# Quadrant products of a two-block transformer kernel issued in rows, inverse transforms in pairs, forward transforms on the whole array

## The chip, the cores and the metric

The kernel runs on one core of a Trainium2 chip, as one launch. The metric is the device time of one execution in microseconds. The core's engines are told by the profile's names: PE (matrix products; PEld is its weight load), DVE (elementwise on vectors), ACT (activations), POOL, and SP, whose queue issues the weight loads.

## What is computed

512 tokens of 1024 features pass two blocks. The first is a conformer convolution (a product to 2048 columns with a gate, a depthwise convolution of width 31 inside segments of 64 tokens, a layer norm, a second product) and an MLP. The second has two layers: differential attention with a Fourier mix in layer 0, a short convolution in layer 1, and behind each a mixture of 16 experts, in which every expert takes its best 64 tokens.

```python
def rms_norm(x, g):
    xf = x.astype(jnp.float32)
    y = xf * lax.rsqrt(jnp.mean(xf * xf, axis=-1, keepdims=True) + EPS)
    return (y * g.astype(jnp.float32)).astype(x.dtype)
...
    u = dwconv(u.reshape(B * n_seg, L // n_seg, D), w_dw).reshape(B, L, D) + b_dw
    u = jax.nn.silu(layer_norm(u, ln_g, ln_b))
    return u @ w_pw2 + b_pw2
...
    aff = jax.nn.softmax(h.astype(jnp.float32) @ w_router.astype(jnp.float32), axis=-1)
    g, idx = lax.top_k(aff.swapaxes(1, 2), cap)
    xs = jax.vmap(lambda hb, ib: hb[ib])(h, idx)
    a = jax.nn.silu(jnp.einsum('becd,edf->becf', xs, w_gate)) * jnp.einsum('becd,edf->becf', xs, w_up)
    y = jnp.einsum('becf,efd->becd', a, w_down) * g[..., None].astype(h.dtype)
...
        x = x + g_m * y
        x = x + g_f * ec_moe(modulate_2(x, norm_ffn[l], sh_f, sc_f),
                             router_w[l], moe_w_gate[l], moe_w_up[l], moe_w_down[l])
```

The norms are over all 1024 features of a token; h of the router is the normed x.

## The kernel before

The activations are kept as X, 128 partitions by 8 feature blocks f by 512 tokens, so a sum over features is a sum over partitions and blocks. A framework orders the instructions of each engine from the program's text and its buffers; each engine works through its own row in that order, and waits by semaphores.

Dense products are three products each (`mm3`, L442 to L444): weight and input are split into a high and a low part by ACT (L435) and DVE (L436). They work on halves of the tokens, 256 columns, in most stages (L442, `128x256`), and on 512 columns in the convolution's.

A sum of squares over features (`sumsq`) is made of eight squares by ACT (`square`, L349; tile `sq`, four buffers) and eight products on PE (L351) with a block of 32 columns of ones. Block f goes to quadrant 32 * (f % 4) of the PSUM tile `sm`, so that four products in a row lie in four different quadrants. It is called in the second norm of block 1 (both halves), the norm of layer 0 (both halves, with 32 weighted columns in place of ones) and the norm of layer 1 (both halves).

In the output product of each layer (`mix_out`) each block of 128 features is added to X by DVE (L730) as soon as its dense product is done, and behind it `route_stat` adds to the token statistics of the router: a product of X with the router's weights (L1235, 32 columns, tile `wrg`) and the product of a square (L351), both in quadrant f % 4. Four groups of four blocks follow each other: half 0 of the tokens with f 0 to 3, then 4 to 7, then half 1. Behind half 0's last block `route_half` makes the router's softmax and, on DVE, the top-k (L1278 to L1281).

In `conv_half` (called for two halves of 256 tokens) the depthwise convolution is a transform: for each of four pieces (two tiles of 128 tokens, two halves of 512 features) PE transforms the two segments of 64 tokens (L690, a tile of 64 rows and 119 columns: the first segment in rows 0 to 63, the second in rows 64 to 127), DVE multiplies by the filter's transform (L693), and PE transforms back (L696, 119 rows, 64 columns: segment b into columns 64 * b of one tile). All these, and the squares' and router's products, are f32 and show as two MATMULs each in the trace.

The experts' weights are loaded through one queue of SP (L1411) into buffers that come free as PE's expert products (L1426) are done.

Of the kernel before, what the change touches and what calls it, by code (L numbers as in the profile page):

```python
# [153 lines left out]
class _Net:  # L154
# [173 lines left out]
    def sumsq(self, xs, t0, n, w=None):  # L328


        nc = self.nc
        ps = self.sm_ps()
        for f in range(KT):
            self.square(ps[:, :n], xs, f, t0, n, f < 4, f >= 4, None if w is None else w[:, f])
        s = self.tmp.tile([128, 256], F32, name="sqs", tag="sqs", bufs=1)
        nc.vector.tensor_copy(s[:, :n], ps[:, :n])
        m = 1 if w is None else 2
        for t in range(n // 128):
            nc.tensor.matmul(ps[:, 256 + m * t:256 + m * t + m], s[:, 128 * t:128 * t + 128],
                             self.cst("quad" if w is None else "quad2"), start=True, stop=True,  # L340
                             skip_group_check=True)
        out = ps[:, 256:256 + m * n // 128]
        return out if w is None else out.rearrange("p (t m) -> p t m", m=2)

    def square(self, ps, xs, f, t0, n, start, stop, w=None):

        nc = self.nc
        s = self.tmp.tile([128, 256], F32, name="sq", tag="sq", bufs=4)
        nc.scalar.activation(s[:, :n], xs[:, f, t0:t0 + n], AF.Square)  # L349
        q = 32 * (f % 4)  # L350
        nc.tensor.matmul(ps[q:q + 32], self.cst("ones")[:, :32] if w is None else w, s[:, :n], start=start, stop=stop,  # L351
                         skip_group_check=True)

    def rsqrt(self, ms, n, tag="rs"):

# [317 lines left out]
    def conv_half(self, hf, u, gf, bdw, zh, zl):  # L673

        nc = self.nc
        fo = _CO["dft"][0]
        cv = self.page().rearrange("p (t d) -> p t d", t=2)
        for i in range(2):
            t = 2 * hf + i

            sm = self.sml.tile([128, 3], F32, name="lns", tag="lns")
            prt = self.page()
            pr = prt[:119].rearrange("p (b d) -> p b d", b=2)
            for h in range(2):
                c = slice(512 * h, 512 * h + 512)
                ps = []
                for b in range(2):
                    p = self.mm_ps()
                    o, q = fo + 119 * b, slice(64 * b, 64 * b + 64)
                    nc.tensor.matmul(p[:119], self.cs[q, o:o + 119], u[q, t, c], start=True, stop=True)  # L690
                    ps.append(p)
                for b in range(2):
                    nc.vector.tensor_tensor(pr[:, b, c], ps[b][:119], gf[:, c], op=ALU.mult)  # L693
                o = self.sm_ps()
                for b in range(2):
                    nc.tensor.matmul(o[64 * b:64 * b + 64], self.cst("idft", 119), pr[:, b, c],  # L696
                                     start=True, stop=True, skip_group_check=True)
                nc.vector.tensor_tensor_reduce(cv[:, i, c], o, bdw[:, c], 1.0, 0.0 if h == 0 else sm[:, 0:1],
                                               ALU.add, ALU.add, sm[:, h:h + 1])

            nc.vector.tensor_scalar(sm[:, 1:2], sm[:, 1:2], -1.0 / D, None, op0=ALU.mult)
            nc.scalar.activation(prt[:, :D], cv[:, i], AF.Square, bias=sm[:, 1:2], accum_out=sm[:, 2:3])
            nc.vector.tensor_scalar(sm[:, 2:3], sm[:, 2:3], 1.0 / D, None, op0=ALU.mult)
            r = self.rsqrt(sm[:, 2:3], 1, tag="ln")
            nc.vector.tensor_scalar(cv[:, i], cv[:, i], sm[:, 1:2], r, op0=ALU.add, op1=ALU.mult)
            if i == 1:

                nc.scalar.activation(sm[:, 0:1], r, AF.Silu)
        for f0 in range(0, KT, 2):
            ps = self.sm_ps()  # L710
            for j in range(2):
                f = f0 + j
                for i in range(2):
                    o = 256 * j + 128 * i
                    nc.tensor.transpose(ps[:, o:o + 128], cv[:, i, 128 * f:128 * f + 128], self.cst("ident"))
            for j in range(2):
                f = f0 + j
                s = self.tmp.tile([128, T], F32, name="sl", tag="sl", bufs=2)
                nc.scalar.activation(s[:, :256], ps[:, 256 * j:256 * j + 256], AF.Silu,
                                     bias=self.vec("conv_ln_b", f), scale=self.vec("conv_ln_g", f))  # L720
                self.split(zh[:, f], zl[:, f], s[:, :256])
        if hf == 1:
            with self.logs_table():
                nc.scalar.copy(self.sml.tile([128, 1], F32, name="done0", tag="lns1"), s[:, :1])
# [438 lines left out]
    def mix_out(self, l, src, xh, xl, key, w=None, last_head=False):  # L1163

        if w is None:
            w = list(self.pieces(self.wload(src[:, :512])))
        src = [src[:, :512], src[:, 512:]]
        mids = [None] * 4
        if last_head:

            w = w[:2] + w[3:] + w[2:3]
            mids[0] = lambda: self.head_norm(5, self.sm_ps())
        route = self.stop >= 7 + 2 * l
        if route:
            self.lg, self.sqb = self.sm_ps(), self.sm_ps()
            chain = [self.route_half(t0, n) for t0, n in self.AB]
            r = []
            mids[2] = lambda: r.append(next(chain[0]))

        for i in range(4):  # L1180
            add = self.add_to_x(self.mods[key], 4 * (i % 2))

            def ev(j, ps, gi, t0, n):
                add(j, ps, gi, t0, n)
                if route:
                    self.route_stat(4 * (i % 2) + j, t0, n)

            nxt = self.wload(src[(i + 1) % 2]) if i < 3 else []
            it = []
            self.dense_f(w, self.groups(xh, xl, self.AB[i // 2:i // 2 + 1]), ev, mids[i],  # L1190
                         lambda: it.extend(self.pieces(nxt)))
            w = it
            if route and i == 2:
                next(chain[0])
        if route:
            r.append(next(chain[1]))
            next(chain[1])
            next(chain[0], None)
            for i in range(2):
                self.token_major(*self.AB[i], r[i])  # L1200
            next(chain[1], None)
        self.dump("d_y%d" % l, self.X)
# [27 lines left out]
    def route_stat(self, f, t0, n):  # L1230

        q = 32 * (f % 4)
        ts = slice(t0, t0 + n)
        first = f < 4 and t0 == 0
        self.nc.tensor.matmul(self.lg[q:q + 32, ts], self.wr[:, f], self.X[:, f, ts], start=first, stop=(f >= 4),  # L1235
                              skip_group_check=True)
        self.square(self.sqb[:, ts], self.X, f, t0, n, first, f >= 4)

    def route_half(self, t0, n):

# [177 lines left out]
    def product(self, name, l, j, lhs, mid=None):  # L1418

        ps = [self.mm_ps(), self.mm_ps()]  # L1420
        for k in range(KT):
            if k % 2 == 0:
                w = [self.eload(self.rows(name, l, j + 8 * b)[:, k:k + 2]) for b in range(2)]
            for n in range(2):
                for b in range(2):
                    self.pe(self.nc.tensor.matmul(ps[n][64 * b:64 * b + 64], lhs[:, k, 64 * b:64 * b + 64],  # L1426
                                                  w[b][k % 2][:, 512 * n:512 * n + 512],
                                                  start=(k == 0), stop=(k == KT - 1), skip_group_check=True))
            if mid and k < 6:
                mid(k)  # L1430
        return ps
# [203 lines left out]
```

## Time and profile before

| | before |
|---|---|
| median of 3 runs | 2148.46 us (2144.57 to 2150.37) |
| profiled execution | 2149.96 us |
| its span | 2148.2 us |
| mean granted clock of PE | 0.984 |
| PE busy | 2043.2 us, 95% |
| DVE busy | 1004.7 us, 47% |
| ACT busy | 558.5 us, 26% |
| moved by DMA | 581.26 MB |

The span is the profiled execution from its first to its last instruction; busy times are of that one execution. The median is over executions without a profile. A granted clock of 1.00 is the full clock of PE.

### The profile page before, as it was taken

Reading aid. Unit: us, or ns where it says so; the run is one execution under the profiler, and the core shown is the slowest. Engines: PE = TensorE matmul, PEld = TensorE weight load, DVE = VectorE, ACT = ScalarE, POOL = GpSimd, SP = SyncE. Lnnn points to the kernel's source line nnn. Section 1 sums busy time; section 2 is a strip of 40 time slices with the busy share of each in tenths; the row PEclk is TensorE's granted clock in tenths of the full one; section 3 lists DMA queues with packets and bytes.
Section 4 is the critical chain, followed back from the end, with each engine's and each line's share of the span. In section 5 each row is a group of like instructions: output and inputs, shape, how many; then the busy total and the mean of one; then the engine's idle time right before and its main releaser. Section 6 shows DMA issues by size and latency. Waiting matters only on the chain. (4 is left out here: it accounts for less than half of the span.)

```text
span 2148.2 us, 26989 instructions
## 1 busy us (share of the span) xinstructions
PE 2043.2 (95%) x10986; PEld 1353.0 (63%) x10986; DVE 1004.7 (47%) x1998; ACT 558.5 (26%) x1035; POOL 18.0 (1%) x20
## 2 busy tenths in 40 slices
PE   6999999999999989989999999979998999999998
PEld 4758888788888978865444434428887544444443
DVE  3878995787575469661222212235356122121221
ACT  3344534243343359630000000023233000000001
POOL 0000000000000000000000000010000000000000
PEclk8999999999999999999999999989999999999999
DMA  9726486588411253448999999992254799999997
GB/s 357 260 80 214 168 292 184 189 290 257 151 47 33 81 142 94 173 161 321 411 420 421 421 421 421 420 356 68 97 215 157 293 404 421 421 421 420 421 421 279
DMA packets 157979, 581.26 MB, mean 271 GB/s; under 512 B 12385, under 2 KB 21505, under 8 KB 111008
## 3 DMA queue, kind: packets, MB, share of 16 engines
q1 hardware_dynamic: 157344, 579.00, 70.7%
q8 instruction: 86, 1.41, 0.3%
q10 hardware_dynamic: 320, 0.52, 0.1%
q14 instruction: 37, 0.30, 0.0%
q0 software_dynamic: 192, 0.03, 0.0%
HBM read 571.50 MB, written 2.11 MB: 267 GB/s over the span
## 5 line engine op out<-in xcount | busy, mean ns | idle before, releaser
L442 PE MATMUL mm<-b,wh 128*128 128x512 f32 (+1 forms) x1136 | 391.4, 346 | 0.6 <-ACT ao L1138 0.5
L443 PE MATMUL mm<-b,wh 128*128 128x512 f32 (+1 forms) x1136 | 391.6, 345 | 0.0
L444 PE MATMUL mm<-b,wl 128*128 128x512 f32 (+1 forms) x1136 | 388.2, 343 | 0.0
L1426 PE MATMUL mm<-w,xs 128*64 128x512 f32 x1152 | 263.8, 600 | 13.2 <-DMA w<-w_u 13.2
L436 DVE TENSOR_TENSOR wl<-w,wh 128x1024 fp32r<-128x1024 f32 x160 | 194.1, 1221 | 168.2 <-ACT wh L435 167.0
L435 ACT CAST wh<-w 128x1024 fp32r<-128x1024 f32 x164 | 170.4, 1049 | 341.7 <-PE mm L443 264.4
L442 PEld LDWEIGHTS mm<-b,wh 128*128 128x128 f32 x1136 | 215.6, 190 | 39.2 <-issue 10.4
L443 PEld LDWEIGHTS mm<-b,wh 128*128 128x128 f32 x1136 | 216.0, 190 | 33.9 <-issue 8.7
L444 PEld LDWEIGHTS mm<-b,wl 128*128 128x128 f32 x1136 | 215.4, 190 | 27.5 <-issue 2.9
L1444 DVE TENSOR_TENSOR ea<-mm,ea 128x512 f32<-128x512 f32 x32 | 22.1, 691 | 395.8 <-PE mm L1426 348.9
L1426 PE MATMUL mm<-b,xs 128*64 128x512 f32 x864 | 198.4, 594 | 3.7 <-DMA b<-w_u 3.5
L1426 PEld LDWEIGHTS mm<-w,xs 128*64 128x64 f32 x1152 | 84.7, 138 | 175.1 <-issue 140.3
L249 DVE SCALAR_TENSOR_TENSOR w<-w,sc 128x512 f32<-128x512 f32 x252 | 184.0, 748 | 4.9 <-DMA w<-ada_w 1.6
L1426 PEld LDWEIGHTS mm<-b,xs 128*64 128x64 f32 x864 | 69.0, 137 | 123.8 <-issue 102.2
L1381 PEld LDWEIGHTS sm<-o,b 128*128 128x128 f32 x1024 | 118.8, 194 | 34.8 <-DVE o L1370 16.0
L1381 PE MATMUL sm<-o,b 128*128 128x128 f32 x1024 | 126.3, 282 | 13.8 <-DVE o L1370 13.8
L1473 DVE SCALAR_TENSOR_TENSOR yl<-mm,scol,yh 128x512 fp32r<-128x512 f32 x30 | 22.5, 751 | 213.2 <-ACT yh L1472 211.5
L442 PE MATMUL mm<-wh,b 128*128 128x512 f32 (+1 forms) x320 | 116.1, 366 | 2.6 <-ACT wh L435 2.6
L443 PE MATMUL mm<-wl,b 128*128 128x512 f32 (+1 forms) x320 | 116.5, 364 | 0.0
L444 PE MATMUL mm<-wh,b 128*128 128x512 f32 (+1 forms) x320 | 116.2, 363 | 0.0
L1426 PE MATMUL mm<-w,eaT 128*64 128x512 f32 x512 | 112.7, 594 | 1.9 <-ACT eaT L1457 1.9
L1440 ACT ACTIVATE ea<-mm 128x512 f32<-128x512 f32 x32 | 19.1, 597 | 343.2 <-PE mm L1426 343.2
(342 smaller groups left out, 2389.0 us busy)
## 6 DMA issues: line engine op xcount, KB each, us to landing
w<-w_g SPq DMA_DIRECT2D x80, 1024.0 KB, 19.8
w<-w_d SPq DMA_DIRECT2D x64, 1024.0 KB, 17.7
w<-w_u SPq DMA_DIRECT2D x64, 1024.0 KB, 19.8
b<-w_u SPq DMA_DIRECT2D x60, 1024.0 KB, 19.8
w<-ada_w SPq DMA_DIRECT2D x48, 1024.0 KB, 5.8
b<-w_g SPq DMA_DIRECT2D x48, 1024.0 KB, 19.8
b<-w_d SPq DMA_DIRECT2D x48, 1024.0 KB, 19.8
w<-w SPq DMA_DIRECT2D x32, 1024.0 KB, 7.2
```

Source lines behind the costliest of these rows:

```text
L249: nc.vector.scalar_tensor_tensor(acc, w[:, i], sc, acc, op0=ALU.mult, op1=ALU.add)
L435: self.nc.scalar.copy(vh, w[:, i:i + kp])
L436: (lo or self.nc.vector).tensor_tensor(vl, w[:, i:i + kp], vh.bitcast(F32), op=ALU.subtract)
L442: mm(out, sh, mh, start=start, stop=False)
L443: mm(out, sh, ml, start=False, stop=False)
L444: mm(out, sl, mh, start=False, stop=stop)
L1381: self.pe(nc.tensor.matmul(ps[:, 128 * i:128 * i + 128], self.xn[:, t, 128 * k:128 * k + 128], o[:, t], start=(t == 0), stop=(t == 3), ski ...
L1426: self.pe(self.nc.tensor.matmul(ps[n][64 * b:64 * b + 64], lhs[:, k, 64 * b:64 * b + 64], w[b][k % 2][:, 512 * n:512 * n + 512], start=(k ...
L1440: nc.scalar.activation(av[:, :, 64 * n:64 * n + 64], gp[n].rearrange("p (q k) -> p k q", k=KT), AF.Silu)
L1444: nc.vector.tensor_tensor(av[:, :, c], up[n].rearrange("p (q k) -> p k q", k=KT), av[:, :, c], op=ALU.mult)
L1473: self.nc.vector.scalar_tensor_tensor(yl[:, c], ps, w, yh[:, c].bitcast(F32), op0=ALU.mult, op1=ALU.subtract)
```

## The change

Three edits. `square` no longer issues its product but returns it as a function; a new method `beside` issues a list of products, the last first, and pins each behind the one before, so that they stand in one row on PE. `sumsq` hands it four squares' products at a time; `route_stat` collects four router products and four squares' products and hands over all eight with the fourth block. The two inverse transforms of a piece go through `beside` too, so the second segment's comes first. And the forward transform of a segment uses all 128 rows of the array: its constant is already laid out as two diagonal blocks with zeros beside them, so the other segment's rows are multiplied by zeros.

```diff
--- before.py
+++ after.py
@@ -330,8 +330,12 @@
 
         nc = self.nc
         ps = self.sm_ps()
+        qs = []
         for f in range(KT):
-            self.square(ps[:, :n], xs, f, t0, n, f < 4, f >= 4, None if w is None else w[:, f])
+            qs.append(self.square(ps[:, :n], xs, f, t0, n, f < 4, f >= 4, None if w is None else w[:, f]))
+            if f % 4 == 3:
+                self.beside(qs)
+                qs = []
         s = self.tmp.tile([128, 256], F32, name="sqs", tag="sqs", bufs=1)
         nc.vector.tensor_copy(s[:, :n], ps[:, :n])
         m = 1 if w is None else 2
@@ -348,8 +352,15 @@
         s = self.tmp.tile([128, 256], F32, name="sq", tag="sq", bufs=4)
         nc.scalar.activation(s[:, :n], xs[:, f, t0:t0 + n], AF.Square)
         q = 32 * (f % 4)
-        nc.tensor.matmul(ps[q:q + 32], self.cst("ones")[:, :32] if w is None else w, s[:, :n], start=start, stop=stop,
-                         skip_group_check=True)
+        return lambda: nc.tensor.matmul(ps[q:q + 32], self.cst("ones")[:, :32] if w is None else w, s[:, :n],
+                                        start=start, stop=stop, skip_group_check=True)
+
+    def beside(self, products):
+
+        for i, product in enumerate(products[::-1]):
+            ins = product()
+            if i:
+                self.tc.keep_in_program_order(ins)
 
     def rsqrt(self, ms, n, tag="rs"):
 
@@ -686,15 +697,15 @@
                 ps = []
                 for b in range(2):
                     p = self.mm_ps()
-                    o, q = fo + 119 * b, slice(64 * b, 64 * b + 64)
-                    nc.tensor.matmul(p[:119], self.cs[q, o:o + 119], u[q, t, c], start=True, stop=True)
+                    o = fo + 119 * b
+                    nc.tensor.matmul(p[:119], self.cs[:, o:o + 119], u[:, t, c], start=True, stop=True)
                     ps.append(p)
                 for b in range(2):
                     nc.vector.tensor_tensor(pr[:, b, c], ps[b][:119], gf[:, c], op=ALU.mult)
                 o = self.sm_ps()
-                for b in range(2):
-                    nc.tensor.matmul(o[64 * b:64 * b + 64], self.cst("idft", 119), pr[:, b, c],
-                                     start=True, stop=True, skip_group_check=True)
+                self.beside([lambda b=b: nc.tensor.matmul(o[64 * b:64 * b + 64], self.cst("idft", 119), pr[:, b, c],
+                                                          start=True, stop=True, skip_group_check=True)
+                             for b in range(2)])
                 nc.vector.tensor_tensor_reduce(cv[:, i, c], o, bdw[:, c], 1.0, 0.0 if h == 0 else sm[:, 0:1],
                                                ALU.add, ALU.add, sm[:, h:h + 1])
 
@@ -1173,6 +1184,7 @@
         route = self.stop >= 7 + 2 * l
         if route:
             self.lg, self.sqb = self.sm_ps(), self.sm_ps()
+            self.rq4, self.sq4 = [], []
             chain = [self.route_half(t0, n) for t0, n in self.AB]
             r = []
             mids[2] = lambda: r.append(next(chain[0]))
@@ -1232,9 +1244,12 @@
         q = 32 * (f % 4)
         ts = slice(t0, t0 + n)
         first = f < 4 and t0 == 0
-        self.nc.tensor.matmul(self.lg[q:q + 32, ts], self.wr[:, f], self.X[:, f, ts], start=first, stop=(f >= 4),
-                              skip_group_check=True)
-        self.square(self.sqb[:, ts], self.X, f, t0, n, first, f >= 4)
+        self.rq4 += [lambda: self.nc.tensor.matmul(self.lg[q:q + 32, ts], self.wr[:, f], self.X[:, f, ts], start=first,
+                                                   stop=(f >= 4), skip_group_check=True)]
+        self.sq4 += [self.square(self.sqb[:, ts], self.X, f, t0, n, first, f >= 4)]
+        if f % 4 == 3:
+            self.beside(self.rq4 + self.sq4)
+            self.rq4, self.sq4 = [], []
 
     def route_half(self, t0, n):
 
```

Line 442 of before is line 453 after, 351 is 355, 1235 is 1247, 690 is 701, 696 is 706.

On PE, in the first set of the route statistics of layer 0 (L442 to L444 and L453 to L455 are dense products, L351 and L355 squares' products, L1235 and L1247 router products), before:

```order
L444 MATMUL mm<-b_5853,wl 128x256
L1235 MATMUL sm<-X,wrg 32x256
L351 MATMUL sm<-sq,cs 32x256
L1235 MATMUL sm<-X,wrg 32x256 x2
L442 MATMUL mm<-b_5853,wh 128x256
L1235 MATMUL sm<-X,wrg 32x256
L443 MATMUL mm<-b_5854,wh 128x256
L444 MATMUL mm<-b_5853,wl 128x256
L442 MATMUL mm<-b_5853,wh 128x256
L351 MATMUL sm<-sq,cs 32x256
L443 MATMUL mm<-b_5854,wh 128x256
L444 MATMUL mm<-b_5853,wl 128x256
```

and after:

```order
L453 MATMUL mm<-b_5853,wh 128x256
L454 MATMUL mm<-b_5854,wh 128x256
L355 MATMUL sm<-sq,cs 32x256 x4
L1247 MATMUL sm<-X,wrg 32x256 x4
L455 MATMUL mm<-b_5853,wl 128x256
L453 MATMUL mm<-b_5853,wh 128x256
L454 MATMUL mm<-b_5854,wh 128x256
L455 MATMUL mm<-b_5853,wl 128x256
```

The eight products have moved into one row, which begins 17 dense products later than the first of them stood; before, they stood between the dense products of the next stage.

On PE, in the first half of the convolution (L690 and L701 forward, L696 and L706 inverse transforms), before:

```order
L444 MATMUL mm<-wh,b_164 128x512
L690 MATMUL mm<-b_392,cs 119x512 x4
L696 MATMUL sm<-w,cs 64x512 x4
L690 MATMUL mm<-b_392,cs 119x512 x3
L696 MATMUL sm<-w,cs 64x512 x2
L690 MATMUL mm<-b_392,cs 119x512
L696 MATMUL sm<-w,cs 64x512 x2
L442 MATMUL mm<-wh,b_163 128x512
```

and after:

```order
L455 MATMUL mm<-wh,b_164 128x512
L701 MATMUL mm<-b_392,cs 119x512 x5
L706 MATMUL sm<-w,cs 64x512 x4
L701 MATMUL mm<-b_392,cs 119x512 x3
L706 MATMUL sm<-w,cs 64x512 x4
L453 MATMUL mm<-wh,b_163 128x512
```

One more forward transform stands ahead of the first inverse ones, and the last two inverse pairs have come together.

On DVE, at the end of layer 0's output product (L1278, L1281 and L1293, L1296 are the top-k, L730 and L741 the additions to X, L1285 and L1300 a cast of the top-k's indices), before:

```order
L1281 MAX_INDEX ix<-gt,at 16x8
L1278 MAX gt<-at 16x8
L730 SCALAR_TENSOR_TENSOR X<-mm,m_gm,X 128x256
L1281 MAX_INDEX ix<-gt,at 16x8
L730 SCALAR_TENSOR_TENSOR X<-mm,m_gm,X 128x256
L1285 CAST gt<-ix 16x64
L730 SCALAR_TENSOR_TENSOR X<-mm,m_gm,X 128x256 x2
```

and after:

```order
L1296 MAX_INDEX ix<-gt,at 16x8
L1293 MAX gt<-at 16x8
L1296 MAX_INDEX ix<-gt,at 16x8
L741 SCALAR_TENSOR_TENSOR X<-mm,m_gm,X 128x256
L1300 CAST gt<-ix 16x64
L741 SCALAR_TENSOR_TENSOR X<-mm,m_gm,X 128x256 x3
```

The first addition to X of these four has moved behind the top-k's last instruction.

## Rows read from the trace of the kernel before

**Rows 1.** The page's busy totals (busy us, share of the span, instructions).
```profile
PE 2043.2 (95%) x10986; PEld 1353.0 (63%) x10986; DVE 1004.7 (47%) x1998; ACT 558.5 (26%) x1035; POOL 18.0 (1%) x20
```

**Rows 2.** Stretches: length, engines' busy us, granted clock, DMA share, GB/s.
```profile
885.00:945.00 60.00, 60.00 (x445) 51.31 (x446) 36.72 (x90) 20.57 (x36) 0.00 (x0) 1.00 0.45 159
...
960.00:975.00 15.00, 10.51 (x51) 6.28 (x52) 6.11 (x23) 1.46 (x2) 0.00 (x0) 0.77 0.01 1
...
1000.00:1400.00 400.00, 383.73 (x1984) 177.51 (x1982) 82.73 (x153) 25.49 (x42) 0.92 (x2) 1.00 1.01 417
```

**Rows 3.** Waits of SP's queue, 940 to 1000 us (us, times, longest).
```profile
SPq L1411 <- PE mm L1426: 44.6, 6, 26.6
```

**Rows 4.** PE's timeline, norm 2, first half (start, us, ..., count, [idle before]).
```profile
208.84 0.28 PE L444 MATMUL mm<-w,wl 128*128 128x256 f32 x1
209.04 0.64 PE L351 MATMUL sm<-sq,cs 128*32 128x256 f32 x8
...
209.84 0.28 PE L443 MATMUL mm<-b,wh 128*128 128x256 f32 x1
...
212.62 0.62 PE L351 MATMUL sm<-sq,cs 128*32 128x256 f32 x2
...
213.39 0.28 PE L443 MATMUL mm<-b,wh 128*128 128x256 f32 x1
```

**Rows 5.** PE's timeline, second half of norm 2.
```profile
227.59 0.93 PE L351 MATMUL sm<-sq,cs 128*32 128x256 f32 x4 [0.96 <-ACT sq L349]
```

**Rows 6.** PE's timeline, one set of the route statistics, layer 0, half 0.
```profile
896.75 0.28 PE L443 MATMUL mm<-b,wh 128*128 128x256 f32 x1
896.87 0.28 PE L444 MATMUL mm<-b,wl 128*128 128x256 f32 x1
897.08 0.81 PE L1235 MATMUL sm<-X,wrg 128*32 128x256 f32 x5
...
898.07 0.38 PE L442 MATMUL mm<-b,wh 128*128 128x256 f32 x1
...
902.32 0.28 PE L443 MATMUL mm<-b,wh 128*128 128x256 f32 x1
```

**Rows 7.** PE's timeline, second norm of layer 1.
```profile
1447.66 1.08 PE L351 MATMUL sm<-sq,cs 128*32 128x256 f32 x8
...
1449.57 1.74 PE L351 MATMUL sm<-sq,cs 128*32 128x256 f32 x6
...
1452.81 1.06 PE L351 MATMUL sm<-sq,cs 128*32 128x256 f32 x2
```

**Rows 8.** DVE's timeline, last blocks of layer 0's output product.
```profile
943.22 0.48 DVE L730 SCALAR_TENSOR_TENSOR X<-mm,m_gm,X 128x256 f32<-128x256 f32 x1 [2.23 <-PE mm L444]
```

**Rows 9.** PE's timeline, both halves of the convolution.
```profile
126.61 1.12 PE L690 MATMUL mm<-b,cs 64*119 64x512 f32 x4
128.90 1.12 PE L690 MATMUL mm<-b,cs 64*119 64x512 f32 x4 [1.17 <-DVE b L616]
...
134.80 1.73 PE L696 MATMUL sm<-w,cs 119*64 119x512 f32 x4
...
139.36 0.50 PE L442 MATMUL mm<-wh,b 128*128 128x512 f32 x1
...
156.46 1.12 PE L690 MATMUL mm<-b,cs 64*119 64x512 f32 x4 [2.61 <-DVE b L616]
...
167.33 0.39 PE L442 MATMUL mm<-w,wh 128*128 128x256 f32 x1
...
169.31 1.21 PE L696 MATMUL sm<-w,cs 119*64 119x512 f32 x4
```

**Rows 10.** PE's timeline, attention of layer 0, full-array f32 products.
```profile
770.68 4.48 PE L1076 MATMUL s<-w,b 128*128 128x256 f32 x20
```

**Rows 11.** Busy time from 158 to 160 us, columns as in rows 2.
```profile
158.00:160.00 2.00, 2.00 (x4) 0.48 (x4) 2.00 (x3) 0.08 (x1) 0.00 (x0) 0.55 1.04 400
```

**Rows 12.** The page's group of ACT's weight casts (busy us, mean ns).
```profile
L435 ACT CAST wh<-w 128x1024 fp32r<-128x1024 f32 x164 | 170.4, 1049 | 341.7 <-PE mm L443 264.4
```

## Prediction

> **What bounds the kernel now.** I read the page's busy totals first: PE is busy 95% of the span, DVE and ACT far less [rows 1]. Such a share is an average, so I went to the stretches in which the edited lines stand. Across the first output product, where layer 0's router work lies, PE was busy all of 60.00 us; DVE, ACT and DMA were not [rows 2]. There every microsecond that PE spends on something else delays the end. The opposite stretch is the experts: from 1000 to 1400 us DMA's share is 1.01, so DMA sets the pace [rows 2]. Does time won ahead of it survive? From 960 to 975 us DMA's share is 0.01 [rows 2]: it stands still, and the queue that issues the loads waits 44.6 us in all for PE's expert products to free buffers [rows 3]. So the DMA-bound stretch hangs on PE's progress and starts earlier when PE arrives earlier; layer 1 is built the same way. I count PE time won before the experts in full.
>
> **What a quadrant product costs.** A square's product uses 32 of the array's columns. Each shows as two MATMULs in the trace, and eight in a row took 0.64 us, as long as two (0.62 us) [rows 4]: products in different quadrants run side by side, and a single one pays the whole visit. Dense matmuls of 256 columns start 0.12 us apart (896.75 and 896.87 in [rows 6]). From 208.84 to 209.84 is 1.00 us with two dense steps: a visit of four costs 1.00 - 0.24 = 0.76. From 208.84 to 213.39 there are eleven dense steps and eight products: 4.55 - 1.32 = 3.23. Two groups of four would be 1.52. **This half-norm gains 1.7.**
>
> **Other sums of squares.** The half-norms of layer 0 (two) show the same spread visits, and I give each 1.7. The second half of norm 2 has them too, and a stall: PE idled 0.96 us for a square by ACT [rows 5]. If the group hides it, 2.7 are won, if it meets it again 1.7: I take 2.2. In layer 1's second half PE ran slowly: 1.74 + 1.06 us where a row of eight took 1.08 [rows 7], so 1.7. First halves that are already in a row gain nothing. Sum 1.7 + 3.4 + 2.2 + 1.7 = **9.0**.
>
> **Route statistics.** One set is four feature blocks of one half of the tokens: four squares and four router products, now interleaved with dense work. From 896.87 to 902.32 is 5.45 us with eleven dense steps: 5.45 - 1.32 = 4.13 for eight products [rows 6]. After, the order has them in one row. The price of that: the two kinds share quadrants, so they can't all run beside each other. The visit from 896.87 to 898.07 has four products, two of them in one quadrant: 1.20 less one dense step of 0.12 is 1.08, for two rounds in the fullest quadrant, as the group of eight has. At the most it is two groups of four, 1.52. I take 1.3, the middle, since the visit has half as many products. Each set gains 4.13 - 1.3 = 2.8; there are three such sets a layer that read alike, six in all: 17.0. The fourth set of each layer comes when PE has no dense work of the stage left to delay; there I count nothing. At that place DVE can take something back. Today it idles 2.23 us for PE, from 940.99, before it adds a block of the last four to X [rows 8]; until then it works on half 0's top-k, which the two sets of half 0 hold up. With them top-k ends 5.6 earlier, at 935.4, but PE is three sets, 8.5 us, earlier, and would need DVE at 943.22 - 8.5 = 934.7. DVE is then up to 0.7 late. I charge 0.4 a layer, between 0 and 0.8. **16.2** in all.
>
> **The convolution.** Two edits of opposite sign. The inverse pair now mostly runs serially: 1.73 us for two products (four MATMULs) at 134.80 [rows 9], where a pair side by side with its visit took 1.21 (at 169.31). One product of 512 columns is 1.73 / 2 = 0.865, so a visit costs 1.21 - 0.865 = 0.35 on top. The forward pair now runs side by side: 1.12 us for two (at 126.61). With all 128 rows of the array it can't: a full-array f32 product shows 4.48 / 20 = 0.22 per 256 columns [rows 10], 0.88 for 512, so a pair becomes 1.73.
>
> - Half 0 takes 126.61 to 139.36, 12.75 us, with PE idle 1.17 for DVE's block at 128.90 [rows 9]. After: eight forward products 8 x 0.865 = 6.9; four inverse pairs in two visits, 4 x 0.865 + 2 x 0.35 = 4.2; the third transform is ready 2.29 us after the start and now two products cover 1.73 of it, so 0.56 idle. 11.7: gain 1.1.
> - Half 1 takes 156.46 to 167.33, 10.87 [rows 9]. After: six forward products (5.2) and two pairs (2.4), 7.6; the other two pairs go into the dense work, one visit (1.21) more there than now. Gain 10.87 - 7.6 - 1.2 = 2.1. But the granted clock was 0.55 from 158 to 160 us, between the levels 1.2 and 2.4 GHz, after PE had idled 2.61 us for DVE [rows 9, 11]; that idling stays, and if the clock falls again some 1.7 is lost: 0.4. I take 0.9, nearer to the low end.
>
> Sum **2.0**. Bounds: if only the forward edit counted, eight pairs times 0.865 lost, -6.9; if all eight inverse pairs are serial now and won 1.73 - 1.21, with forward transforms covered by the waits for DVE, +4.2.
>
> The Trainium skill speaks against this edit: "TensorEngine Tiling (Array Packing)", Performance Considerations, says that a contraction of 64 rows or fewer is when to tile rows, two at once. The trace agrees that two ran at once (1.12 us for two [rows 9]). By that rule alone the sum would take the -6.9 and end at 2130; the same page's Key Properties say that a change of tiling mode drains the array, which no row here isolates.
>
> **Sum.** 9.0 + 16.2 + 2.0 = 27.2. The profiled execution took 2149.96 us, span 2148.2; 2149.96 - 27.2 = 2122.8. It lies 1.5 above the median of the runs, 2148.46, so against that 2121.3: **2121**.
>
> **What hides nothing and what waits.** SP's and POOL's orders are unchanged, so no transfer moves past another. The change does add a wait: a group begins only when its last square is there, and all dense matmuls behind it on PE wait too, since PE goes in order. Today PE waits 0.96 us once [rows 5]. By the order the first set's group comes 17 dense matmuls later than its first product did, some 17 x 0.12 = 2.0 us, in which the squares behind that one are made: that is the cover; without it each of the 13 new rows (five priced norms, eight router sets) pays.
>
> **The rivals.**
> - Forward transforms lose what they cost and inverse ones win nothing: -6.9 in place of +2.0, gain 18.3, 2130. For it: 1.12 against 1.73 [rows 9]. Against: half 0's sum above has the gaps and serial pairs to pay with. 0.13.
> - Groups stall: 13 x 0.96 = 12.5 given back, gain 14.7, 2134. For it [rows 5]; against, ACT has time between (20.57 of 60.00 us busy [rows 2]). 0.06.
> - Slower: squares queue on ACT behind weight casts of 1049 ns [rows 12]. From 27.2 / 13 = 2.1 us a group, two casts ahead of the last square, nothing is left; three casts, 3.1 us, give 13 x 3.1 = 40.3 against 27.2, 2162. PE would idle before most groups, and it is 100% busy today with casts and squares on the same queue. 0.03.
> - No change: the experts' DMA stretch, at 1.01, takes all that was won, as it would if its start hung on something other than PE. Against: DMA's 0.01 just before it. 2148, 0.08 (a gain up to 6 counts here).
> - As summed: 0.70, with its own range 2112 to 2130 from the conv bounds (-6.9, +4.2) and the group's 1.08 to 1.52.
>
> **Numbers.** About 0.3%, 6 us, is what a measurement can tell. Faster: 0.70 + 0.13 + 0.06 = 0.89; same 0.08; slower 0.03. The range takes in the bounds and the conv rival and part of the stall rival: 2110 to 2133; outside lie no change, slower and some of the stalls, under 0.2.
>
> **What the profile after should show.** Router sets as one group of 16 MATMULs of some 1.2 us and a dense matmul right behind; some 13 fewer microseconds of visits from 885 to 945; the dense work after conv half 0 starting near 1 us earlier, after half 1 two to three; the first expert product some 20 us earlier, and DMA's stretch moved as much. I am wrong if PE shows idle time released by ACT's squares before the groups, if forward products take more than 0.9 us each, or if the experts start earlier and end at the same time.

## The result and the profile after

The changed kernel takes 2124.02 us (median of 4 runs, 2122.97 to 2125.66), against 2148.33 for before in the same comparison: a ratio of 0.9885, 95% interval 0.9873 to 0.9898. That is 24.3 us less. The profiled execution took 2124.88 us with a span of 2123.1.

The page's busy totals, in the form of [rows 1]:

```profile
PE 2015.2 (95%) x10986; PEld 1347.0 (63%) x10986; DVE 1003.8 (47%) x1998; ACT 559.2 (26%) x1035; POOL 18.0 (1%) x20
```

PE has the same 10986 instructions and is busy 28.0 us less; DVE and ACT are where they were. The stretches of [rows 2], moved with the work, in the same columns:

```profile
885.00:930.00 45.00, 44.34 (x388) 41.75 (x386) 31.82 (x80) 16.89 (x30) 0.00 (x0) 1.00 0.45 156
960.00:975.00 15.00, 15.00 (x84) 8.19 (x84) 2.19 (x6) 0.00 (x0) 0.00 (x0) 1.00 0.98 364
...
1000.00:1400.00 400.00, 379.82 (x1944) 171.88 (x1940) 80.75 (x148) 26.96 (x44) 0.92 (x2) 1.00 1.01 417
```

From 960 to 975 us, where DMA stood still before (0.01), its share is now 0.98: the experts' loads have begun. The stretch behind it runs at the same 417 GB/s. SP's queue still waits for PE's expert products, as in [rows 3] (920 to 990 us, same columns):

```profile
SPq L1426 <- PE mm L1441: 46.4, 7, 26.7
```

PE's timeline at the set of the route statistics that answers to [rows 6] (start, us, line, tile, shape, count):

```profile
891.72 0.28 PE L454 MATMUL mm<-b,wh 128*128 128x256 f32 x1
891.93 0.64 PE L355 MATMUL sm<-sq,cs 128*32 128x256 f32 x8
892.39 0.61 PE L1247 MATMUL sm<-X,wrg 128*32 128x256 f32 x8
892.93 0.39 PE L455 MATMUL mm<-b,wl 128*128 128x256 f32 x1
893.15 0.28 PE L453 MATMUL mm<-b,wh 128*128 128x256 f32 x1
```

All 16 MATMULs stand in one row. From 891.72 to 893.15 is 1.43 us with two dense steps of 0.12: the set costs 1.19, where it cost 4.13. A product that stood alone before paid 0.74: from the line below to 213.39 [rows 4] is 0.98 us with two dense steps.

```profile
212.41 0.28 PE L444 MATMUL mm<-b,wl 128*128 128x256 f32 x1
```

PE's timeline in both halves of the convolution, for [rows 9]:

```profile
128.23 1.88 PE L701 MATMUL mm<-b,cs 128*119 128x512 f32 x4
130.60 2.83 PE L701 MATMUL mm<-b,cs 128*119 128x512 f32 x6 [0.50 <-DVE b L627]
133.37 1.94 PE L706 MATMUL sm<-w,cs 119*64 119x512 f32 x8
135.23 2.83 PE L701 MATMUL mm<-b,cs 128*119 128x512 f32 x6
138.00 1.94 PE L706 MATMUL sm<-w,cs 119*64 119x512 f32 x8
139.87 0.50 PE L453 MATMUL mm<-wh,b 128*128 128x512 f32 x1
...
153.14 1.88 PE L701 MATMUL mm<-b,cs 128*119 128x512 f32 x4
156.97 4.55 PE L701 MATMUL mm<-b,cs 128*119 128x512 f32 x10 [1.95 <-DVE b L627]
161.45 1.08 PE L706 MATMUL sm<-w,cs 119*64 119x512 f32 x4
...
164.52 0.39 PE L453 MATMUL mm<-w,wh 128*128 128x256 f32 x1
```

A full-array forward product takes 1.88 / 2 = 0.94 us, 2.83 / 3 the same. Two inverse pairs in a row (x8) take 1.94 us, 0.97 a pair, where a pair took 1.73 alone. Half 0 goes from 128.23 to 139.87, 11.64 us; before it was 12.75.

Why a pair ran serially before can be read on DVE, whose products with the filter feed the two inverse products one after the other. For the pair at 134.80 [rows 9]:

```profile
134.05 0.69 DVE L693 TENSOR_TENSOR w<-mm,b 119x512 f32<-119x512 f32 x1 [0.29 <-PE mm L690]
134.72 1.28 DVE L693 TENSOR_TENSOR w<-mm,b 119x512 f32<-119x512 f32 x2
```

The first inverse product started at 134.80, as soon as its input was there; the second's input was done at 135.40, and it started at 135.46. With the second segment's product first, both inputs are there when the pair begins.

PE's timeline in the second half of norm 2, for [rows 5], and the stretches behind it (columns as above; the third value from the end is the granted clock):

```profile
224.90 0.28 PE L454 MATMUL mm<-b,wh 128*128 128x256 f32 x1
226.17 0.64 PE L355 MATMUL sm<-sq,cs 128*32 128x256 f32 x8 [0.99 <-ACT sq L353]
227.57 0.39 PE L455 MATMUL mm<-b,wl 128*128 128x256 f32 x1 [0.77 <-DVE wl L447]
```

```profile
228.00:230.00 2.00, 2.00 (x12) 2.00 (x11) 1.84 (x3) 0.47 (x2) 0.00 (x0) 0.50 0.54 117
230.00:232.00 2.00, 2.00 (x13) 2.00 (x13) 2.00 (x7) 0.00 (x0) 0.00 (x0) 0.65 1.06 403
```

Here something is given back. PE waits 0.99 us for a square as before, then 0.77 us for DVE's low part of a weight, which it had not waited for, and then the granted clock is 0.50, the lower level of 1.2 GHz, to beyond 231 us.

It is not the only group that waits for a square. All waits of PE for squares in the whole span (us, times, longest), before and after:

```profile
PE sm L351 <- ACT sq L349: 1.0, 1, 1.0
```

```profile
PE sm L355 <- ACT sq L353: 4.1, 5, 1.1
```

**Where the time came from.** Each dense product of before has its partner in the other kernel. I took the start of the k-th high-by-high product (L442, and its line in the other kernels) in both traces; before's start less the other's is the lead there, and how far the lead grows across a section is what that section gained. All values are us gained on the profiled execution of before, read from one execution of each kernel, so a few tenths mean little; the columns with one edit belong to the experiments below.

| section | predicted | changed | only routes (e1) | only norms (e2) | only conv (e3) | only inverse (e5) | only forward (e6) |
|---|---|---|---|---|---|---|---|
| first dense product | 0 | -1.9 | -1.6 | 1.0 | -2.7 | 0.2 | 1.8 |
| convolution, half 0 | 1.1 | 1.2 | 0.0 | 0.0 | 1.2 | 2.3 | -0.2 |
| convolution, half 1 | 0.9 | 3.4 | 0.0 | 0.8 | 3.3 | 3.5 | 0.1 |
| norm 2, to the next norm | 3.9 | 1.1 | 0.0 | 1.6 | -2.1 | -1.2 | 0.0 |
| norm of layer 0 | 3.4 | 2.8 | 0.0 | 2.8 | 0.0 | 0.0 | 0.0 |
| routes, layer 0 | 8.1 | 8.6 | 8.6 | 0.0 | 0.0 | 0.0 | 0.0 |
| norm of layer 1 | 1.7 | 1.6 | 0.1 | 1.8 | 1.9 | 1.8 | 1.8 |
| routes, layer 1 | 8.1 | 8.6 | 8.6 | 0.0 | 0.0 | 0.0 | 0.0 |
| all other | 0 | -0.3 | -1.1 | 0.0 | 0.5 | 0.7 | 2.0 |
| span | 27.2 | 25.1 | 14.5 | 8.0 | 2.1 | 7.1 | 5.4 |

The first line is not the change's: the work ahead of the first dense product (36.13 us before, 37.99 after) is the same, and its length differs from execution to execution (see the last section). Without it the span gained 26.9. The medians differ by 24.3. In half 1 of the convolution the granted clock also differed between these executions: it stayed at 1.00 in the changed kernel, e2, e3 and e6, and was 0.50 for 3.4 us in before, e1 and e5. So the 0.8 of e2, whose convolution is that of before, is not the work of an edit.

### The profile page after: what moved, and what is told of

Its sections match the earlier page's. It is cut to its first block, busy times and chain, and to the rows that moved or that the text cites. A ratio compares the mean times of both kernels' runs of the same rounds, so it can differ in the third digit from the quotient of the medians.

```text
span 2123.1 us, 26986 instructions
## 1 busy us (share of the span) xinstructions
PE 2015.2 (95%) x10986; PEld 1347.0 (63%) x10986; DVE 1003.8 (47%) x1998; ACT 559.2 (26%) x1035; POOL 18.0 (1%) x20
## 5 line engine op out<-in xcount | busy, mean ns | idle before, releaser
L453 PE MATMUL mm<-b,wh 128*128 128x512 f32 (+1 forms) x1136 | 389.7, 345 | 1.6 <-ACT b L407 1.1
L455 PE MATMUL mm<-b,wl 128*128 128x512 f32 (+1 forms) x1136 | 388.9, 344 | 0.8 <-DVE wl L447 0.8
L453 PEld LDWEIGHTS mm<-b,wh 128*128 128x128 f32 x1136 | 215.8, 191 | 35.5 <-issue 5.0
L455 PEld LDWEIGHTS mm<-b,wl 128*128 128x128 f32 x1136 | 216.3, 191 | 27.8 <-issue 2.5
L453 PE MATMUL mm<-wh,b 128*128 128x512 f32 (+1 forms) x320 | 115.9, 365 | 2.6 <-ACT wh L446 2.6
L455 PE MATMUL mm<-wh,b 128*128 128x512 f32 (+1 forms) x320 | 116.0, 362 | 0.0
## 6 DMA issues: line engine op xcount, KB each, us to landing
w<-w_d SPq DMA_DIRECT2D x64, 1024.0 KB, 17.8
```

The lines of the kernel that those rows point to most:

```text
L453: mm(out, sh, mh, start=start, stop=False)
L455: mm(out, sl, mh, start=False, stop=stop)
```

## The experiments

**Only the routes (e1).** From the changed kernel, the norms and the convolution go back.

```diff
-            if f % 4 == 3:
-                self.beside(qs)
+            self.square(ps[:, :n], xs, f, t0, n, f < 4, f >= 4, None if w is None else w[:, f])()
...
+                    nc.tensor.matmul(p[:119], self.cs[q, o:o + 119], u[q, t, c], start=True, stop=True)
...
+                for b in range(2):
+                    nc.tensor.matmul(o[64 * b:64 * b + 64], self.cst("idft", 119), pr[:, b, c],
```

> Only the route statistics go in rows of eight; sums of squares, inverse and forward transforms as before. Theory 1 (a visit of PE to quadrant products has a price of its own, and the sets of a stage add up): six sets fall from 4.14 us to the 1.2 us that the changed kernel shows, six times 2.95 is 17.7, less 0 to 1.4 that DVE or the experts take back, so 16 to 18 us faster, near 2131. Rival (the gain depends on the other edits arriving early, or the experts' DMA stretch swallows part when it comes alone): under 13 us faster, above 2135.

Measured: 2132.66 against 2149.12, ratio 0.9920 (0.9903 to 0.9937). The two layers gain 8.6 each, as in the changed kernel. The routes stand alone and the experts don't swallow them.

**Only the norms (e2).** `sumsq` in groups of four, the rest as before.

> Only the sums of squares go in rows of four; the rest as before. Theory 1 (the prediction's sum): 9.0 us faster, 2139. Rival, from the trace of the changed kernel: the second half of norm 2 gives back what it wins, since PE waits there 0.99 us for a square and 0.77 us for DVE and then runs 3 us at half the clock; then 1.7 + 2.9 + 1.6 less 0 to 1, so 5 to 6 us faster, 2142 to 2143, with that wait and low clock seen in the trace between 225 and 236 us. A second rival: the wait was due to the lead that the convolution had given PE over DVE; alone, norm 2 then wins 2 us and the whole 8 to 9.

Measured: 2141.05 against 2149.12, ratio 0.9962 (0.9949 to 0.9976). The trace shows what the first rival named: PE waits 0.9 us for a square and 0.7 us for DVE in norm 2's second half and then runs at the lower clock, without any lead from the convolution. So the second rival falls in its reason, though the median's 8.1 us lies in its 8 to 9. By the sections the norms themselves gained 6.2 (1.6 + 2.8 + 1.8), a little over the first rival's 5 to 6; most of the rest is the start (1.0) and the clock in half 1 of the convolution (0.8).

**Only the convolution (e3).** The two transform edits, the rest as before.

> Only the two edits of the convolution; the rest as before. Prediction's sum: 2.0 us faster (bounds -6.9 to +4.2). From the leads in the changed kernel's trace: 1.4 in the first half of the convolution and 3.4 in the second, 4.8 us faster at 185 us. Theory 1: these survive to the end, 2143.5. Rival: DVE, which is busy nine tenths of the stretch 220 to 300 us, takes them back, and the end moves by less than 2 us.

Measured: 2146.67 against 2149.12, ratio 0.9985 (0.9976 to 0.9995). The lead of 4.5 is won in the two halves, and norm 2's section takes 2.1 of it back: PE waits 1.7 us for DVE there, where before has none of these waits (0.7 at 196.4 us, 0.5 at 230.5 and 0.5 at 231.6). The rival named the right engine, though the first wait lies ahead of its stretch; half survives.

**Forward transforms back on 64 rows (e4), all else as changed.**

```diff
-                    o = fo + 119 * b
-                    nc.tensor.matmul(p[:119], self.cs[:, o:o + 119], u[:, t, c], start=True, stop=True)
+                    o, q = fo + 119 * b, slice(64 * b, 64 * b + 64)
+                    nc.tensor.matmul(p[:119], self.cs[q, o:o + 119], u[q, t, c], start=True, stop=True)
```

> The changed kernel with the forward transforms back on tiles of 64 rows, two segments side by side; inverse pairs, norms and routes as changed. Theory 1 (a full-array forward product costs 0.86 us, two side by side 1.12, and the rest of the stage has no slack): 8 pairs at 0.61 each, up to 4.9 us faster than the changed kernel, 2119 to 2122. Rival (what the forward edit pays is covered or returned, because mixing 64-row tiles with full-array work costs a change of mode at each switch and keeps pairs waiting): no faster than the changed kernel, 2124 or above by up to 4.

Measured: 2123.74, ratio to before 0.9881 (0.9866 to 0.9896), the same as the changed kernel. Half 0 gains 2.3 in place of 1.2; half 1 loses 0.9, since there the granted clock stood at 0.50 from 155 to 168 us. By the median, theory 1 is wrong; in half 0 the edit is worth 1.1 us, under half of theory 1's four pairs at 0.61.

**Only the inverse pairs (e5).**

> Only the inverse pair is issued in a row, the second segment first; forward transforms on 64 rows, norms and routes as before. Theory 1 (inverse pairs run serially in the kernel before and side by side in a row): each serial pair falls from 1.73 to 1.1 us, half 0 of the convolution gains 3 us (3.4 in the run with 64-row forward transforms), half 1 up to 2 more where the clock stays at its higher level, 2144 to 2146. Rival (the two edits need each other, or the pairs only wait elsewhere): within 1 us of before.

Measured: 2145.48 against 2149.23, ratio 0.9989 (0.9979 to 0.9999). PE's timeline, half 0:

```profile
130.64 2.17 PE L702 MATMUL sm<-w,cs 119*64 119x512 f32 x8
...
134.65 1.08 PE L702 MATMUL sm<-w,cs 119*64 119x512 f32 x4
```

A pair in a row takes 1.08 where it took 1.73 [rows 9]. With 2.3 and 3.5 us in the two halves, this edit alone carries more than the whole convolution's gain in the changed kernel (1.2 and 3.4).

**Only the forward transforms (e6).**

> Only the forward transforms use all 128 rows; inverse pairs, norms and routes as before. Theory 1: 8 pairs go from 1.12 to 1.73 us and up, 2 to 5 us slower at the end of the convolution, 2151 to 2154, unless half 1's clock stays at its higher level where the kernel before shows 3.4 us at 0.50 to 0.70 (1.7 us back). Rival, from the change (the fuller array work is what wins in half 1): 1 to 3 us faster.

Measured: 2148.13 against 2149.23, ratio 1.0004 (0.9992 to 1.0015): no difference. The halves give -0.2 and 0.1. Neither the loss of 2 to 5 us nor the gain came. The clock in half 1 stayed at 1.00, which alone brought e2 0.8 there; at equal clock the full-array transforms lost some 0.7.

**Without the pins (e7).** The changed kernel, with

```diff
-            if i:
-                self.tc.keep_in_program_order(ins)
```

> The changed kernel without the pins: products are still issued behind the fourth square, the last first, but the scheduler may place each; by its order four of the six sets that matter stand as two rows of four, three to five dense products apart. Theory 1 (the visit has the price, the row of eight shares it): a set in two rows costs 1.52 in place of 1.20, four times 0.32 is 1.3 us slower than the changed kernel, 2125 to 2126. Rival (the gain hangs on the pins): back by more than 5 us, over 2129.

Measured: 2123.80, ratio to before 0.9885 (0.9871 to 0.9899); the median can't tell it from the changed kernel. PE's timeline shows the price of two rows:

```profile
904.08 0.28 PE L453 MATMUL mm<-b,wl 128*128 128x256 f32 x1
904.29 0.64 PE L1245 MATMUL sm<-X,wrg 128*32 128x256 f32 x8
904.86 0.38 PE L451 MATMUL mm<-b,wh 128*128 128x256 f32 x1
...
905.53 0.64 PE L355 MATMUL sm<-sq,cs 128*32 128x256 f32 x8
906.10 0.39 PE L452 MATMUL mm<-b,wh 128*128 128x256 f32 x1
906.32 0.28 PE L453 MATMUL mm<-b,wl 128*128 128x256 f32 x1
```

904.08 to 906.32 is 2.24 with six dense steps: 1.52, twice 0.76. Four sets times 0.33 is the 1.3 expected. What counts is that the products are issued together; the pins are the last 0.33 of a set's 2.9.

**Another order inside the row (e8).** Square's and router's product of one quadrant next to each other.

```diff
-            self.beside(self.rq4 + self.sq4)
+            self.beside([p for rs in zip(self.rq4, self.sq4) for p in rs])
```

> The changed kernel with the eight products of a set in another order inside the row: the square's and the router's product of one quadrant next to each other, then the next quadrant. Theory 1 (products run side by side only while the next in the row goes to another quadrant; one in the same quadrant waits and holds up those behind it): four waits inside the row, a set costs about 2 us in place of 1.20, six times 0.8 is 5 us slower, 2129. Rival (only the fullest quadrant's two rounds count, in whichever order): 1.2 us a set, the time of the changed kernel.

Measured: 2122.88, ratio to before 0.9889 (0.9871 to 0.9906). PE's timeline at the same set:

```profile
885.16 0.28 PE L454 MATMUL mm<-b,wh 128*128 128x256 f32 x1
885.37 0.66 PE L355 MATMUL sm<-sq,cs 128*32 128x256 f32 x8
885.83 0.64 PE L1247 MATMUL sm<-X,wrg 128*32 128x256 f32 x8
...
886.62 0.28 PE L453 MATMUL mm<-b,wh 128*128 128x256 f32 x1
```

885.16 to 886.62 less two steps is 1.22, against 1.19. My theory of waits inside the row falls; the rival holds: this order inside the row costs no more.

**One half of the convolution each (e9, e10).** Forward transforms on 64 rows in half 0 only (e9, shown), or in half 1 only (e10, with `hf == 1`).

```diff
+                    o, q = fo + 119 * b, slice(64 * b, 64 * b + 64) if hf == 0 else slice(0, 128)
+                    nc.tensor.matmul(p[:119], self.cs[q, o:o + 119], u[q, t, c], start=True, stop=True)
```

> The changed kernel with forward transforms on 64 rows in the first half of the convolution and on 128 rows in the second. Theory 1 (in the first half the full-array transforms only cost; in the second they keep PE busy enough that its clock stays at the higher level): the first half gains 2.3 us in place of 1.1 and the second 3.3 as in the changed kernel, 1.2 us faster, 2122 to 2123, which the median can't tell; the lead over before, counted from the first dense product to the end of the convolution, is 5.6 to 6.0 us in place of 4.7. Rival (the halves hang together): no more than 4.7.

> The changed kernel with forward transforms on 128 rows in the first half of the convolution and on 64 in the second. Theory 1: after its wait for DVE of 2.6 us in the second half the granted clock falls to 0.50 for 3 us or more, as in four of the five kernels so far with 64 rows and in none of five with 128; the second half gains 3.5 us at most, and under 0 if the clock stays low as long as in the run with all forward transforms on 64 rows. Rival (those falls were chance): clock 1.00 throughout 150 to 170 us, and the second half gains 5 us or more.

Measured: e9 2124.12, ratio to before 0.9881 (0.9865 to 0.9898); e10 2125.22, ratio 0.9893 (0.9876 to 0.9909). Neither median can be told from the changed kernel's. The stretch from 156 to 158 us of e9, with 128 rows there, and then of e10, with 64:

```profile
156.00:158.00 2.00, 2.00 (x4) 0.93 (x3) 2.00 (x3) 0.68 (x1) 0.00 (x0) 0.50 0.93 340
```

```profile
156.00:158.00 2.00, 1.53 (x8) 0.80 (x9) 2.00 (x4) 2.00 (x3) 0.00 (x0) 1.00 0.55 94
```

It is the other way round from what I expected: the clock fell with 128 rows and stayed up with 64. So my theory of the clock falls, and e9 gains 2.3 and 1.7, not 5.6 to 6.0. That this is under the rival's 4.7 is the clock's doing: half 0 gains the 2.3 of e4 whatever stands in half 1. PE's timeline of e10 in half 1 shows why the 64 rows win little there even at full clock:

```profile
156.47 2.83 PE L701 MATMUL mm<-b,cs 64*119 64x512 f32 x10 [2.62 <-DVE b L627]
160.63 1.08 PE L706 MATMUL sm<-w,cs 119*64 119x512 f32 x4 [1.33 <-DVE w L704]
```

Five products take 2.83 in place of 4.55, and PE then waits 1.33 us for DVE's product with the filter. Half 1 gains 3.8 so, against 3.4 with 128 rows; the rival's 5 or more did not come either. Where the clock was at 0.50 for 3.4 us in this half, 64 rows still gained 3.5 (e5) and 128 rows 1.7 (e9).

**Norm 2's second half one by one (e11), all else as changed.**

```diff
+            if xs is self.X and w is None and t0 and not self.late:
+                qs.pop()()
```

> The changed kernel with the squares' products of norm 2's second half issued one by one as before; all other groups as changed. Theory 1 (there DVE sets the pace: PE waits for DVE's split of the weights whatever it does with the products): the lead over before changes by no more than 1 us between 226 and 245 us, as with the group (-0.7 to +0.9), and the median is that of the changed kernel. Rival (the group is worth its visits there too, and only the low clock hid it): 2.2 us slower at 245 us than the changed kernel would be at full clock, PE waiting for nothing there.

Measured: 2123.54, ratio to before 0.9881 (0.9864 to 0.9897), as the changed kernel. From the end of the convolution to the norm of layer 0 it gains 0.1, where e8 and e10, grouped and with the clock at 1.00 there, gain 2.6 and 2.7, and the changed kernel, grouped at the lower clock, 1.1. The waits of PE from 205 to 250 us (us, times, longest), first e11, then e8:

```profile
PE mm L457 <- DVE wl L449: 0.5, 1, 0.5
PE sm L345 <- DVE sqs L342: 0.5, 1, 0.5
```

```profile
PE sm L355 <- ACT sq L353: 1.0, 1, 1.0
PE mm L455 <- DVE wl L447: 0.8, 1, 0.8
```

Theory 1 holds in that PE waits for DVE there in both, and e11's lead doesn't change from 226 to 245 us. But the group is worth some 2.1 us when the clock doesn't fall: counted from 200 us, ahead of the norm, to the norm of layer 0, e8 gains 2.9 and e11 0.8. That is the size of the rival, though only 0.9 of it is there by 245 us, and PE did wait for DVE.

## Why the prediction was right

- **PE sets the pace and its lead goes through the experts.** Right. The changed kernel leads by 15.90 us at the first expert product and by 15.54 at 1407.98 us of before's time, 440 us later; e8 by 22.2 and 21.6. Counted from the first dense product the 15.90 is 17.8, near the 17.4 of the sum's terms up to there (the "some 20" named for it was more than these). The rival of no change falls with that, and the queue of the loads still waits 46.4 us for PE's expert products. Behind the experts up to 1.9 us of lead is lost (e7, 13.6 to 11.7), in a stretch where the granted clock is 0.50 for a time.
- **The price of a visit.** Right: one row 0.76, two rows 1.52 (e7), as the sum had it. The group of eight was taken at 1.3 and costs 1.19. Why a visit costs this much no run takes apart.
- **Routes, 16.2.** 17.2 came: six sets at 2.9, and 0.2 of the 0.4 a layer that was charged for DVE. In e1 the same 17.2 came alone.
- **Norms, 9.0.** 5.5 came (1.1 + 2.8 + 1.6). The first half of norm 2 was right (1.7 forecast, 1.7 won); the term that failed is its second half, taken at 2.2: it brought -0.3 (the rest of the section, -0.2, lies ahead of the norm). The prediction had weighed only the square's wait there; the wait of 0.77 for DVE and the lower clock came on top. Where the clock stayed at 1.00 (e8) it brought 1.2. The layer 1 term of 1.7 stands: there the lower clock lasted 13.7 us in before, e1, e2 and the changed kernel, from within 1.4 us of the same place in the work, and the section gains 0.1 with single products (e1) and 1.8 and 1.6 with groups. e3, e5 and e6, which leave that norm as it was, gain 1.8 to 1.9 too, but in them the lower clock lasted only 6.8 us.
- **The convolution, 2.0.** 4.6 came, more than the sum's upper bound of 4.2, which had a pair in a row at 1.21; it took 1.08 alone and 0.97 with a second pair behind it. The lower bound of -6.9 was summed wrongly: by its own rows a forward pair loses 1.73 - 1.12 = 0.61, eight of them 4.9.
  Half 0 was right (1.1 and 1.2), though by two errors that cancel: a forward product took 0.91 to 0.94 us in place of 0.865, over the 0.9 that was named as a sign of being wrong, and a pair of inverse ones 0.97 in place of 1.04.
  In half 1 the stage took 156.97 to 164.52, 7.6 as worked out. The charge of 1.2 for one more visit inside the dense work came (the lead falls by 1.1 there), but 0.8 of it was back by 192 us. The 1.2 set aside for the lower clock was not needed, since it stayed at 1.00. That is luck: in e9, with the same code in this half, the clock fell and the half gained 1.7 in place of 3.4.
  Which edit pays is settled: inverse pairs alone gain 5.8, forward transforms alone nothing; with the inverse pairs in place the forward ones cost 1.1 in half 0, and in half 1 they win nothing at either clock (e5, e9, e10). The Trainium skill's rule on 64-row contractions ("TensorEngine Tiling (Array Packing)", Performance Considerations) agrees with the trace on the pair (1.12 against 1.88 us). Going against it costs nothing that the median shows (e4).
- **Groups that stall.** Five did, 4.1 us in all, against one of 1.0 before: this sign of being wrong was met, in a small way. The longest two (1.06 and 1.05) are the fourth sets of the two layers, with no dense product left behind them: in layer 0 the lead is 15.8 at the last dense product and 15.9 at the first expert one. The others stand in norm 2 (0.99), in layer 0's norm (0.26) and in layer 1's (0.73). The rivals that rested on 0.96 or more in each of 13 groups fall.
- **The sum.** 27.2 was forecast and 26.9 came from the first dense product on; but -3.5 in the norms, +2.6 in the convolution and +1.0 in the routes cancel in it, so that the fit is partly luck. The medians show 24.3, 2.9 under the forecast; 1.9 of the profiled gain was lost ahead of the first dense product.

What the experiments point to, 64 rows in half 0, is worth 1.1 us by the sections; e9, which does it, can't be told from the changed kernel. None beats it.

## What to carry to other kernels

Count visits, not products: a small product that stands alone between dense ones pays a whole visit (0.74 here), and with three more beside it in other quadrants the visit costs 0.76. Issue them together as soon as the last is ready, and look behind for the engine that PE then runs into: here waits for DVE took back part of what norm 2 and the convolution had won. Where two edits are bundled, measure each: here the pair in a row carried the convolution, and the other edit moved nothing that the median shows. Of two products that can run side by side, issue the one whose input comes last first; the other then follows without a wait.

## What the runs showed of the hardware

**The lower clock comes and goes with the same code.** e8 and the changed kernel have the same waits in norm 2 (1.0 for a square, 0.8 for DVE). The clock then fell to 0.50 in one and stayed at 1.00 in the other, as this stretch of e8 shows beside the one of the changed kernel above:

```profile
228.00:230.00 2.00, 2.00 (x19) 2.00 (x18) 1.93 (x6) 0.91 (x2) 0.00 (x0) 1.00 1.03 396
```

In half 1 of the convolution it fell in five of thirteen traces (before, e1, e4, e5 and e9, and not in e2, e3, e6, e7, e8, e10, e11 and the changed kernel), always after PE had idled some 2 us or more for DVE (1.95 in e9, 2.6 in the other four), for 3.4 us in four and 13.7 in e4. PE idled as long where it didn't fall (1.95 in the changed kernel, 2.62 in e10). What decides it in one execution stays open.

**The start differs by 5.7 us.** The first dense product, behind code that no edit touches, started between 33.10 (e11) and 38.80 us (e3):

```profile
33.10 1.22 PE L455 MATMUL mm<-wh,b 128*128 128x512 f32 x2 [2.56 <-ACT wh L448]
```

```profile
38.80 0.79 PE L449 MATMUL mm<-wh,b 128*128 128x512 f32 x1 [2.56 <-ACT wh L442]
```

The granted clock goes with it. From 20 to 33 us it was 0.94 in e11 and 0.58 in e3 (columns as above):

```profile
20.00:33.00 13.00, 8.13 (x52) 4.03 (x52) 6.99 (x16) 4.57 (x8) 0.00 (x0) 0.94 1.05 387
```

```profile
20.00:33.00 13.00, 11.79 (x44) 4.49 (x44) 4.92 (x11) 1.75 (x3) 0.00 (x0) 0.58 1.05 387
```

Over the thirteen traces the time at 0.50 ahead of the first dense product is 1.7 us in e11, some 7 in those that start from 34.35 to 35.18, 11 to 12 in those from 35.98 to 37.99, and 17 in those from 38.42 on. The 5.7 us is about as much as the largest of the convolution's edits (5.8), and of the order of the spread of the runs of one kernel (7.2 for the 23 of before beside e5); only leads counted from there tell these edits apart.
